# Two block products of the up projection taken from their own pairs and placed earlier, in a fused two-layer encoder kernel

## The chip, the cores and the metric

One core of a Trainium2 chip runs the whole program in one launch. The metric is the time on the device in microseconds (us); the median of several runs counts. TensorE (PE) does the matrix products and its weight loads (PEld); VectorE (DVE), ScalarE (ACT) and GpSimd (POOL) work element by element; SyncE (SP) and POOL issue the transfers (DMA).

## The reference, cut to what matters

Two layers, each with a mixing part (gated linear attention and softmax attention side by side), an output projection, and a gated feed-forward part with a causal convolution of width 3. The change touches the up projection of the feed-forward part:

```python
D_MODEL = 1024; SEQ = 1024; DEPTH = 2; N_META = 16; CONV_W = 3
D_FF = 128 * (-(-8 * D_MODEL // (3 * 128)))        # 2816

def conv_ffn(x, w_up, conv_w, conv_b, w_down):
    h = x @ w_up                                    # (1040, 1024) @ (1024, 2 * 2816)
    L = h.shape[1]
    hp = jnp.pad(h, ((0, 0), (CONV_W - 1, 0), (0, 0)))
    hc = conv_b
    for j in range(CONV_W):
        hc = hc + hp[:, j:j + L] * conv_w[j]
    u, g = jnp.split(hc, 2, axis=-1)
    return (jax.nn.silu(g) * u) @ w_down

def reference(...):
    ...
    for i in range(DEPTH):
        ...
        h = h + jnp.concatenate([o_gla, o_fox], axis=-1) @ w_out[i]
        h = h + conv_ffn(rms_norm(h, ffn_norm[i]), w_up[i], conv_w[i], conv_b[i], w_down[i])
    return rms_norm(h, final_norm)[:, N_META:]
```

## The kernel before, in words

Activations lie with the features on the partitions: eight tiles of 128 features by 1040 positions. Float32 products are made from three matmuls on split operands (mm3, L222 to L224): high weights by high activations, low weights by high activations, high weights by low activations. A split is a cast on ACT (the high half) and a subtraction on DVE (the low half).

The up projection has 22 pairs of column tiles, u and g of 128 columns each. A pair j is a 2 by 2 block product (two halves of the features, two halves of the 1040 positions), done with seven half-size products p = 1 to 7 in place of eight, with sums and differences of blocks as operands. (j, p) below is product p of pair j, both as in the code: pairs count from 0, so the fourth and fifth pair are 3 and 4. One product is 4 feature blocks by 2 pieces of 260 positions by 3 matmuls.

Three things feed a product.

- Its activation operand X[p], shared by all pairs: 4 blocks, each split by put (ACT at L1096, DVE at L1097). X[1] and X[2] are made while the output projection still runs (first_operand, L1140). The others are made inside the up projection by make_t2 (X[6]), make_t3 (X[7]), make_n4 (X[4], L1225), make_t1 (X[5], L1232 and L1233) and make_b22 (X[3]); the table named before says ahead of which index of the sequence each is written out.
- Its weight operand: up_operand and block_operand load the four weight blocks of a pair (SP, L1045), for pairs below 5 also a sum S1 of two blocks, by a load (L1048) and an accumulating transfer of POOL (L1049); other combinations are made on DVE (L1055). up_split makes the high and low half (ACT L1072, DVE L1073). Products 1 and 2 of pair 2 have a load of their own (L1033), as they come before the rest of their pair. ensure(i) writes out the operands up to four products ahead. Even and odd products take their halves from separate pools of three buffers.
- A PSUM place. There are four, of two banks each. place(j, p) says which one a product that begins an accumulation takes; products 6, 7 and 4 accumulate on that of product 1, product 3 on that of product 5.

evacuate takes the results out: of products 1 and 2, the first to come is copied by ACT into a new tile hu (L1262), and the second is added by DVE (L1261); products 6, 7, 4 are copied by ACT; products 5 and 7, then 3, are added by DVE into hg and hu. After product 3 the pair's convolution follows (ACT L1250, four DVE instructions at L1254, a product at L1285), and a transfer of the result by POOL. hu and the other large tiles come from one list of slots; the slot freed longest ago is lent first.

The order of the products is written out in seq, and PE keeps it; the other engines' instructions are put in order by a scheduler when the program is built, and each engine then works through its list in order. The order starts with products 2 and 1 of pairs 0 to 2, then takes pairs 0 and 1 side by side through 6, 7, 4, 5, 3, then the rest of pair 2, and from pair 3 on

```python
        for j in range(3, NFF - 1):
            seq += [(j, 2), (j, 6), (j, 5), (j, 7), (j + 1, 1), (j, 4), (j, 3)]
```

Of the kernel before, what the change touches and what calls it, by code (L numbers as in the profile page):

```python
# [39 lines left out]
M_GK, M_GQ, M_GV, M_GR, M_REM, M_FQ, M_FK, M_FV, M_WO, M_UP = 0, 2, 4, 8, 12, 13, 17, 21, 25, 33  # L40
# [95 lines left out]
class Kern:  # L136
# [891 lines left out]


    def up_operand(self, lyr, j, p, fw, raws, odd):  # L1030
        if j == 2 and p in (1, 2):
            src = fw.tile([128, 4, 128], F32, tag="raw2", name="raw2")
            self.nc.sync.dma_start(src[:], self.wm[lyr, M_UP + 4][:, 4 * p - 4:4 * p, :])  # L1033
            return self.up_split(src, fw, odd)
        return self.block_operand(self.wm[lyr, M_UP + 2 * j], self.wm[lyr, M_UP + 2 * j + 1], 4, j, p, fw, raws, odd, j < N_DMA_SUM)

# [39 lines left out]
    def ffn_up(self, lyr, mix, hT, pp, fw, halves, o0, during_last):  # L1076
# [22 lines left out]


        seq = [(j, p) for j in range(3) for p in (2, 1)] + [(j, p) for p in (6, 7, 4, 5, 3) for j in range(2)]
        seq += [(2, 6), (2, 5), (2, 7), (3, 1), (2, 4), (2, 3)]
        for j in range(3, NFF - 1):
            seq += [(j, 2), (j, 6), (j, 5), (j, 7), (j + 1, 1), (j, 4), (j, 3)]
        seq += [(NFF - 1, p) for p in (6, 5, 7, 2, 4, 3)]

        def place(j, p):
            if p == 1:
                return 3 if j == 2 else j % 2
            if p == 2:  # L1110
                return 2 if j < 3 else 3
            return 0 if j == 1 else 2
        raws, ops = {}, []

# [122 lines left out]
        def make_b22():  # L1237
# [1 line left out]
            for k in range(4):  # L1239
                put(3, k, highk[k][:, t1])  # L1240
            s.put(*highk)
        before = {1: second_half, 2: make_t2, 7: make_t3, 8: make_n4, 10: make_t1, 12: make_b22}


        st = {}
# [47 lines left out]
        for i, (j, p) in enumerate(seq):  # L1293
            ensure(i)
            if i in before:
                before[i]()
            q = st.setdefault(j, {})
            bank, first = {2: "y", 5: "x", 3: "x"}.get(p, "a"), p in (1, 2, 5)
            if first:
                q[bank] = bank2("up", place(j, p))  # L1300
            ps, w = q[bank], ops[i]
            ops[i] = None
            for k in range(4):
                hi_, lo_ = (X[p][e][k // 2].t[:, k % 2, :] for e in range(2))
                for c in range(2):
                    self.mm3(ps[:, c, :n], w[k], (hi_, lo_), c * n, n, first and k == 0, k == 3, not first)
            evacuate(j, p)
            if j == NFF - 1:
                for x in X.pop(p):
                    s.put(*x)  # L1310
                during_last(p)
# [446 lines left out]
```

## Time and profile before

| | |
|---|---|
| median of 3 runs | 2525.41 us (2525.14 to 2525.87) |
| profiled execution, its own time | 2530.31 us |
| its span, first to last instruction | 2528.4 us |
| PE busy in the span | 2483.1 us (98%) |
| DVE busy | 1771.4 us (70%) |
| ACT busy | 1274.4 us (50%) |
| mean granted TensorE clock | 0.996 of full speed |

Times inside the profile count from the first instruction. In a line of a timeline come start, duration, engine, line of the code, operation, tiles written and read, and in brackets the idle time before it with what ended that. In a line of waits come who waited for whom, the sum in us, how often, and the longest. Matmuls overlap in the pipeline, so the distance from one start to the next, not the duration, is the time that a matmul takes. The up projection of layer 0 starts at 568.65 us, that of layer 1 at 1820.19 us.

### The profile page before, as it was taken

The numbers are of one execution on the slowest core, as the hardware profiler recorded it, in microseconds if no ns is written. First come the engines' busy times: TensorE is split into PE (matmuls) and PEld (weight loads), VectorE is DVE, ScalarE is ACT, GpSimd is POOL, SyncE is SP. The second block draws the span as 40 slices with busy tenths as digits, with TensorE's granted clock in tenths as the row PEclk, the third lists the DMA queues.
The fourth block names the chain that finished last, engine by engine and source line by source line (L and its number), as shares of the span: only waits on it lengthen the run. The fifth ranks groups of instructions, "written<-read, shape, count | busy, mean of one in ns | idle before, by whom it ended". The sixth has DMA issues, their size and how long they took to land.

```text
span 2528.4 us, 47014 instructions
## 1 busy us (share of the span) xinstructions
PE 2483.1 (98%) x18442; PEld 2385.4 (94%) x18442; DVE 1771.4 (70%) x3523; ACT 1274.4 (50%) x2733; POOL 385.0 (15%) x567
## 2 busy tenths in 40 slices
PE   9999999999999999999999999999999999999998
PEld 8999999999999999999999899999999999997786
DVE  7656777769877777853666666777797777777545
ACT  7346666645544445641343566665464444455412
POOL 2023433110000000100211334331100000001002
PEclk9999999999999999999999999999999999999999
DMA  3232124342322224763312222143432222257622
GB/s 132 68 87 74 49 88 132 116 140 77 116 81 80 79 76 137 197 168 110 105 58 69 74 80 78 58 152 107 143 92 93 79 85 76 80 159 187 184 74 72
DMA packets 117965, 259.88 MB, mean 103 GB/s; under 512 B 14816, under 2 KB 32480, under 8 KB 117744
## 3 DMA queue, kind: packets, MB, share of 16 engines
q1 hardware_dynamic: 93408, 181.74, 23.1%
q0 software_dynamic: 22464, 72.84, 10.5%
q8 instruction: 144, 2.36, 0.4%
q10 hardware_dynamic: 1872, 2.31, 0.3%
q14 instruction: 77, 0.63, 0.1%
HBM read 176.24 MB, written 67.81 MB: 97 GB/s over the span
## 4 chain that ended last, share of the span: by engine, by line
PE 78%; DVE 14%; ACT 5%; issue 2%; DMA 1%; SPq 0%; DVEq 0%; ACTq 0%
PE up L224 10%; PE up L222 10%; PE up L223 10%; PE mm L222 7%; PE mm L223 7%; PE mm L224 7%; PE down L222 5%; PE down L223 5%; PE down L224 5%; PE av L720 3%; PE tr L694 2%; DVE S L661 2%; DVE x L1097 1%; ACT P L673 1%; PE S L658 1%
## 5 line engine op out<-in xcount | busy, mean ns | idle before, releaser
L222 PE MATMUL up<-x,hi 128*128 128x260 f32 (+1 forms) x2464 | 699.0, 284 | 3.0 <-ACT x L1096 2.4
L224 PE MATMUL up<-x,hi 128*128 128x260 f32 (+1 forms) x2464 | 698.5, 283 | 3.4 <-DVE x L1097 3.4
L223 PE MATMUL up<-x,lo 128*128 128x260 f32 (+1 forms) x2464 | 697.5, 283 | 0.0
L224 PEld LDWEIGHTS up<-x,hi 128*128 128x128 f32 x2464 | 467.3, 190 | 5.2 <-DVE x L1097 5.2
L222 PEld LDWEIGHTS up<-x,hi 128*128 128x128 f32 x2464 | 466.2, 189 | 4.4 <-ACT x L1096 3.2
L223 PEld LDWEIGHTS up<-x,lo 128*128 128x128 f32 x2464 | 466.4, 189 | 0.1
L1073 DVE TENSOR_TENSOR lo<-raw,hi 128x512 fp32r<-128x512 f32 x364 | 247.8, 686 | 170.3 <-ACT hi L1072 170.3
L222 PE MATMUL mm<-xh,hi 128*128 128x348 f32 (+4 forms) x1056 | 363.2, 344 | 0.0
L224 PE MATMUL mm<-xl,hi 128*128 128x348 f32 (+4 forms) x1056 | 339.9, 322 | 0.0
L223 PE MATMUL mm<-xh,lo 128*128 128x348 f32 (+4 forms) x1056 | 339.5, 321 | 0.0
L1072 ACT CAST hi<-raw 128x512 fp32r<-128x512 f32 x364 | 224.7, 620 | 143.7 <-PE up L224 93.3
L222 PEld LDWEIGHTS mm<-xh,hi 128*128 128x128 f32 x1056 | 199.7, 189 | 5.2 <-issue 4.6
L223 PEld LDWEIGHTS mm<-xh,lo 128*128 128x128 f32 x1056 | 199.7, 189 | 0.7 <-issue 0.7
L224 PEld LDWEIGHTS mm<-xl,hi 128*128 128x128 f32 x1056 | 198.6, 188 | 0.4 <-issue 0.3
L189 ACT CAST hi<-raw 128x512 fp32r<-128x512 f32 (+2 forms) x168 | 97.4, 581 | 183.1 <-PE down L224 108.7
L223 PE MATMUL down<-ah,lo 128*128 128x260 f32 (+1 forms) x528 | 169.2, 320 | 0.9 <-DVE lo L191 0.9
L222 PE MATMUL down<-ah,hi 128*128 128x260 f32 (+1 forms) x528 | 168.7, 319 | 0.0
L224 PE MATMUL down<-al,hi 128*128 128x260 f32 (+1 forms) x528 | 168.5, 319 | 0.0
L673 ACT ACTIVATE P<-S,m 116x460 f32<-116x460 f32 (+2 forms) x224 | 124.8, 561 | 71.1 <-DVE m L661 67.4
L337 DVE TENSOR_TENSOR PT<-tr,PT 116x464 fp32r<-116x464 f32 (+3 forms) x240 | 122.9, 515 | 47.2 <-ACT PT L336 45.6
L1055 DVE TENSOR_TENSOR raw<-raw,raw 128x512 f32<-128x512 f32 x198 | 129.5, 685 | 17.4 <-DMA raw<-in_wd_dram 14.9
L1286 POOL DMA_DIRECT2D actd<-cv x44 | 23.6, 535 | 765.1 <-DVE cv L1285 744.2
(289 smaller groups left out, 5621.6 us busy)
## 6 DMA issues: line engine op xcount, KB each, us to landing
raw<-in_wm_dram SPq DMA_DIRECT2D x326, 256.0 KB, 2.7
raw<-in_wd_dram SPq DMA_DIRECT2D x64, 256.0 KB, 3.9
actd<-cv POOLq DMA_DIRECT2D x22, 520.0 KB, 3.0
actd<-cv POOLq DMA_DIRECT2D x22, 512.0 KB, 2.9
cb<-cd SPq DMA_DIRECT2D x16, 520.0 KB, 4.1
st<-actd SPq DMA_DIRECT2D x14, 520.0 KB, 5.1
st<-actd SPq DMA_DIRECT2D x14, 512.0 KB, 5.5
kA<-kA SPq DMA_DIRECT2D x24, 260.0 KB, 4.1
```

Source lines behind the costliest of these rows:

```text
L189: nc.scalar.copy(hi[:, :n, :], raw[:, :n, :])
L222: nc.tensor.matmul(ps, wh, xh[:, c0:c0 + n], start=first, stop=False, skip_group_check=more)
L223: nc.tensor.matmul(ps, wl, xh[:, c0:c0 + n], start=False, stop=False, skip_group_check=more)
L224: nc.tensor.matmul(ps, wh, xl[:, c0:c0 + n], start=False, stop=last, skip_group_check=more)
L337: nc.vector.tensor_tensor(out=lo, in0=src, in1=hi.bitcast(F32), op=ALU.subtract)
L661: nc.vector.tensor_tensor_reduce(out=S[:rows, :n], in0=S[:rows, :n], in1=cb[:rows, c0:k1], scale=1.0, scalar=(BIG if ci == 0 else m[:rows, ...
L673: nc.scalar.activation(P[:rows, :n], S[:rows, :n], AF.Exp, scale=-1.0, bias=m[:rows, nch - 1:nch], accum_out=(den if nch == 1 else d3[:row ...
L694: nc.tensor.transpose(tr[:w, 3 - j, :rows], P[:rows, o:o + w], id_)
L720: nc.tensor.matmul(av[:, a:b], w.rearrange("p a b -> p (a b)"), x, start=(t == ts[0] and part == 0 and i == 0), stop=(t == last and i == 1))
L1055: nc.vector.tensor_tensor(out=q[out][:, :nk, :], in0=q[a][:, :nk, :], in1=q[b][:, :nk, :], op=op)
L1072: nc.scalar.copy(hi[:, :nk, :], src[:, :nk, :])
L1073: nc.vector.tensor_tensor(out=lo[:, :nk, :], in0=src[:, :nk, :], in1=hi[:, :nk, :].bitcast(F32), op=ALU.subtract)
```

## The change

Product 2 of pairs 3 and 4 is taken out of its place in those pairs and put between products of pairs 0 and 1: (3, 2) ahead of (1, 7), and (4, 2) ahead of (1, 4). From (1, 6) on the order is then (1,6), (0,7), (3,2), (1,7), (0,4), (4,2), (1,4), (0,5), (1,5), (0,3), (1,3), and pairs 3 and 4 go straight from product 3 of the pair before to their product 6. The two products get a weight load of their own (so the same block is loaded again with the pair's other blocks), their accumulation takes place 2, and the table before is moved by one or two indices, so that the operands are written out ahead of the same products as before. For these pairs product 2 is now the one that is copied, and product 1 the one that is added.

```diff
     def up_operand(self, lyr, j, p, fw, raws, odd):
-        if j == 2 and p in (1, 2):
+        if (j, p) in ((2, 1), (2, 2), (3, 2), (4, 2)):
             src = fw.tile([128, 4, 128], F32, tag="raw2", name="raw2")
-            self.nc.sync.dma_start(src[:], self.wm[lyr, M_UP + 4][:, 4 * p - 4:4 * p, :])
+            self.nc.sync.dma_start(src[:], self.wm[lyr, M_UP + 2 * j][:, 4 * p - 4:4 * p, :])
             return self.up_split(src, fw, odd)
...
         seq = [(j, p) for j in range(3) for p in (2, 1)] + [(j, p) for p in (6, 7, 4, 5, 3) for j in range(2)]
+        seq.insert(9, (3, 2))
+        seq.insert(12, (4, 2))
         seq += [(2, 6), (2, 5), (2, 7), (3, 1), (2, 4), (2, 3)]
         for j in range(3, NFF - 1):
-            seq += [(j, 2), (j, 6), (j, 5), (j, 7), (j + 1, 1), (j, 4), (j, 3)]
+            seq += ([(j, 2)] if j > 4 else []) + [(j, 6), (j, 5), (j, 7), (j + 1, 1), (j, 4), (j, 3)]
...
             if p == 2:
-                return 2 if j < 3 else 3
+                return 2 if j < 5 else 3
...
-        before = {1: second_half, 2: make_t2, 7: make_t3, 8: make_n4, 10: make_t1, 12: make_b22}
+        before = {1: second_half, 2: make_t2, 7: make_t3, 8: make_n4, 11: make_t1, 14: make_b22}
```

## The prediction

> **What bounds the kernel now.** I read the page first, then the stretches of the two places that the change touches, then the waits and the instruction timeline inside them.
>
> ```profile
> span 2528.4 us, 47014 instructions
> PE 2483.1 (98%) x18442; PEld 2385.4 (94%) x18442; DVE 1771.4 (70%) x3523; ACT 1274.4 (50%) x2733; POOL 385.0 (15%) x567
> PE 78%; DVE 14%; ACT 5%; issue 2%; DMA 1%; SPq 0%; DVEq 0%; ACTq 0%
> ```
>
> TensorE is the bound of the whole: 98% of the span. So a reordering pays only where PE stands still or runs slowly. The chain that ended last nevertheless has 14% of DVE in it, so somewhere PE waits for DVE. The stretches (their length, then busy time and instruction count of PE, PEld, DVE, ACT, POOL, then granted clock, DMA share, GB/s) say where:
>
> ```profile
> 600.15:620.21 20.06, 17.34 (x123) 16.11 (x121) 18.64 (x30) 11.26 (x19) 0.88 (x1) 0.91 0.32 85
> 1852.61:1872.66 20.05, 17.48 (x122) 16.27 (x121) 18.48 (x30) 11.14 (x19) 0.87 (x1) 0.91 0.31 82
> 640.00:680.00 40.00, 40.00 (x337) 40.00 (x336) 31.92 (x42) 20.03 (x29) 1.96 (x3) 1.00 0.39 124
> ```
>
> The third row is steady state: 40.00 us for some 335 matmuls (the edges count two), 0.1195 us each; a block product is 4 blocks x 2 pieces x 3 = 24 matmuls, so 2.87 us. The first two rows (layer 0, layer 1) run from the first matmul of (0,4) to the first of (1,3): five products (0,4), (1,4), (0,5), (1,5), (0,3), 120 matmuls, which at 2.87 would take 14.35 us and take 20.06 and 20.05. **5.7 us are lost in each layer.** What ended the waits there, and what the clock did:
>
> ```profile
> PEld up L224 <- DVE x L1097: 2.3, 4, 0.9
> PE up L224 <- DVE x L1097: 1.5, 3, 0.7
> PE up L222 <- ACT x L1096: 1.2, 2, 0.8
> ```
>
> ```profile
> 612.47 0.59 PE L224 MATMUL up<-x,hi 128*128 128x260 f32 x1 [0.38 <-DVE x L1097]
> 612.86 0.42 PE L222 MATMUL up<-x,hi 128*128 128x260 f32 x1
> 613.50 0.42 PE L222 MATMUL up<-x,hi 128*128 128x260 f32 x1
> 615.46 0.34 PE L222 MATMUL up<-x,hi 128*128 128x260 f32 x1
> 617.33 0.28 PE L222 MATMUL up<-x,hi 128*128 128x260 f32 x1
> ```
>
> PE waits for x, the high and low halves of the operands that make_n4 and make_t1 build on ACT (L1096) and DVE (L1097). (0,5) ends only at 613.50, and from 612.86 to 615.46 twelve matmuls start 0.217 us apart, at half clock. The row at 617.33 starts (0,3). DVE is the cause; it has no pause until its second hg add:
>
> ```profile
> 590.81 1.28 DVE L1073 TENSOR_TENSOR lo<-raw,hi 128x512 fp32r<-128x512 f32 x2
> 592.02 0.68 DVE L1261 TENSOR_TENSOR hu<-up,hu 128x520 f32<-128x520 f32 x1
> 596.87 1.91 DVE L1225 TENSOR_TENSOR h<-h,h 128x520 f32<-128x520 f32 x3
> 602.97 1.42 DVE L1232 SCALAR_TENSOR_TENSOR h<-h,vec,r 128x520 f32<-128x520 f32 x2
> 615.39 0.68 DVE L1261 TENSOR_TENSOR hg<-up,hg 128x520 f32<-128x520 f32 x1
> 617.53 0.70 DVE L1261 TENSOR_TENSOR hg<-up,hg 128x520 f32<-128x520 f32 x1 [0.86 <-PE up L224]
> ```
>
> In a full queue one TENSOR_TENSOR follows the other every 0.61 us (1.28 - 0.68 = 0.60; 1.91 for three), one of L1232 every 0.67 to 0.74.
>
> **The change part by part.** *Matmuls.* Their number is unchanged. Per layer (3,2) and (4,2), 48 matmuls on x2, which has long been complete, move ahead of (1,7) and (1,4): 2 x 2.87 = 5.74 us of work that needs nothing from the late operands. (0,4) then starts 2.87 and (0,5) 5.74 us later than the data forced before. The hole is 5.7. So PE's gain is 5.74 minus the delay of (0,3), and that is set by DVE.
>
> *DVE.* By the built program's order, 26 instructions at 0.61 and four L1232 at 0.67 stand between the first L1225 and the first hg add: 18.5 us, as the rows give (615.39 - 596.87). After the change 28 and four stand there, since low halves of later products now come earlier: 19.7 us. The start moves as well. The two new low halves wait for weights that are now loaded on their own (L1033), into buffers that come free when the low halves of (0,7) and (1,7) are done:
>
> ```profile
> 591.55 0.33 SPq L1045 DMA_DIRECT2D raw<-in_wm_dram  x1
> 593.33 0.33 SPq L1048 DMA_DIRECT2D raw<-in_wm_dram  x1
> raw<-in_wm_dram SPq DMA_DIRECT2D x4, 256.0 KB, 3.0
> 592.22 0.62 ACT L1072 CAST hi<-raw 128x512 fp32r<-128x512 f32 x1
> 594.61 0.59 ACT L1262 COPY hu<-up 128x520 f32<-128x520 f32 x1 [1.77 <-PE up L224]
> ```
>
> The first load takes the place of the one at 591.55 and lands 3.0 us later, at 594.6; cast to 595.2, low half to 595.9; (3,2) starts at 597.3. Covered. The second follows the low half of (1,7), which ends at 592.7 (it trades places with the hu add at 592.02), and lands at 595.8. On ACT stand two casts and the hu copy before and with it, so its cast ends at 596.8 and its low half at 597.5. DVE has four low halves of x7 and two of weights to do until 596.4, then idles some 0.4: the first L1225 starts at 597.4 instead of 596.87. Bounds: 596.4 if the load is early, and later one for one if it is late. Then the hg add starts at 597.4 + 19.7 = 617.1 and ends at 617.8; (0,3), which accumulates on that bank, starts at 617.85 instead of 617.33.
>
> (0,5): four products after 600.15 it starts at 611.63 and needs its last low half with its 21st matmul, at 614.0. On DVE 21 x 0.61 + 4 x 0.67 = 15.5 stand before that: start 612.9, end 613.5. No wait, by 0.5 us. So both kinds of loss in the hole go, the half clock too, as PE no longer pauses: 5.74 - 0.52 = **5.2 us per layer**; 5.7 if the load is early. The second layer's hole has the same length and the same counts.
>
> [...]
>
> *ACT.* Two hu copies of 0.59 come earlier; for these two pairs the copy now follows product 2 and the DVE add product 1, one of each as before. The copy of (4,2) stands ahead of the cast of the last block of x5. It waits for (4,2), done at 608.9, and for its slot, that of acc, read last by the fourth L1232, done at 609.9. It ends at 610.5, while that cast's input comes only at 611.6. (0,5) reuses the same bank, at 611.63. Nothing, with 1.1 us of cover.
>
> *SP and POOL.* Four loads of 256 KB more in all; DMA share is 0.32 there. They stand ahead of the third pair's loads. Its S1 load (593.33) goes behind the low half of (4,2), to 597.5:
>
> ```profile
> 596.95 0.87 POOL L1049 DMA_DIRECT2D raw<-in_wm_dram  x1 [24.86 <-DMA raw<-in_wm_dram]
> raw<-in_wm_dram POOLq DMA_DIRECT2D x1, 256.0 KB, 4.2
> 611.13 0.68 DVE L1055 TENSOR_TENSOR raw<-raw,raw 128x512 f32<-128x512 f32 x1
> ```
>
> so POOL's accumulation starts near 601 and has landed at 606; DVE takes it at about 612. Nothing, with 6 us of cover.
>
> *What comes after.* Pairs 3 and 4 run without their product 2 between (j,3) and (j,6), so three turnarounds get shorter by 2.87: the hu add before (3,6), and bank 2 from (2,3) to (3,5) and from (3,3) to (4,5). DVE must keep up:
>
> ```profile
> 617.00:632.00 15.00, 15.00 (x127) 15.00 (x127) 13.91 (x15) 9.78 (x12) 0.56 (x1) 1.00 0.17 43
> 632.00:650.00 18.00, 18.00 (x153) 18.00 (x152) 18.00 (x24) 10.95 (x16) 1.98 (x3) 1.00 0.46 141
> 650.00:663.30 13.30, 13.30 (x114) 13.30 (x113) 10.39 (x16) 7.05 (x11) 0.00 (x0) 1.00 0.56 180
> 619.39 1.30 DVE L1254 SCALAR_TENSOR_TENSOR cv<-hg,vec,cv 128x1039 f32<-128x1039 f32 x1 [0.56 <-ACT cv L1250]
> 632.65 0.69 DVE L1073 TENSOR_TENSOR lo<-raw,hi 128x512 fp32r<-128x512 f32 x1
> 634.61 0.28 PE L222 MATMUL up<-x,hi 128*128 128x260 f32 x1
> ```
>
> Before, the low half of (2,4) ends at 633.34, 1.3 us ahead of its product. After, (2,4) starts at about 635.0 (617.85 + 6 x 2.87). From the first L1254 at 619.4 on (the two low halves already made are missing, the convolutions of pairs 0 and 1 are the same, 1.21 each) the built order puts that low half at 633.2 in layer 0 and, with both pairs' convolutions ahead of it, at 634.3 in layer 1: 1.8 and 0.7 us to spare. The same sum gives (2,3) 0.9, and the add that frees bank 2 for (3,5) 0.8. All small, none negative, so I take zero; the upper bound is a rival. Behind 650 DVE idles again (10.39 of 13.30).
>
> Sum: 2 x 5.2 = 10.4 us off 2530.3 (the profiled execution's own time; span 2528.4), so 2519.9 there. The median of the runs shown is 2525.41, 4.9 us lower; the hole is work and waits on engines, so I take the same 10.4 off it: **2515.0**. If all 5.7 come back in each layer, 2514.0. A difference of 0.2%, 5 us, is about what a measurement of this kernel can tell from none.
>
> **The rivals.** *DVE gives part of it back later.* PE reaches (4,6), at 663.3 before, 5.2 us sooner in each layer, with the same DVE work; DVE's idle time from 617 to there is 1.09 + 2.91 = 4.0, most of it at the end. Spare 0.7 to 0.9 at three places is within what my sum can miss: 0.1 us at each of the waits for ACT on the way would be over a microsecond. Price 1 to 2.5 us per layer: 2517 to 2520. Against it: DVE reaches 619.4 no later than before. 0.15.
>
> *The half clock stays.* If the pauses did not cause it, twelve matmuls at 0.217 instead of 0.1195 cost 1.2 us per layer wherever they fall: 2517.4. For it: no pause there is above 0.9 us. Against it: the fall follows four pauses in 5 us, and the stretch without pauses shows 1.00. 0.08. [...]
>
> *Slower: ACT and DVE queue up behind the load of (4,2).* The cast for it stands in front of every cast of x4 and x5, its low half in front of all of make_n4 and make_t1, and DVE has no idle time, so each microsecond beyond 595.8 delays the hole's end by one. It decides at 3.0 + 5.2 = 8.2 us to landing; at 11 us it is 2525.4 + 2 x 2.8 = 2531. Against it: 3.0 in this stretch, two loads at a time. 0.04.
>
> *The products fill nothing,* because (0,5) waits for the bank that (4,2) used, or (0,3) for its add, as long as it waited for x: no change, 2525. 0.04.
>
> **How the numbers follow.** The forecast, 0.69, holds 2513.8 to 2516.5. With the first two rivals the range reaches to 2520, which leaves out 0.08 and the edges. Faster by over 0.2%: forecast, half clock and most of the giving back, 0.89; within it 0.06; slower 0.05.
>
> **What would show it.** Right: between (0,4) and (1,3), now six products, PE waits under 0.5 us and the granted clock stays at 1.00; (0,3) starts near 617.9; the first L1225 near 597.4; no PE wait for lo L1073 or hu L1261 up to (4,6). Wrong: waits of PE for DVE adds L1263 (the same lines, moved by two) or lo L1073 between 630 and 660, or a first L1225 after 599.

## The result

The changed kernel takes 2517.62 us (median of 6 executions, 2515.66 to 2519.32), beside 2525.91 us for the kernel before in the same comparison (6 executions, 2525.14 to 2527.37): ratio 0.9966, 95% interval 0.9954 to 0.9979. It is faster by some 8.6 us, within 5.3 to 11.6. The profiled execution of the changed kernel took 2517.71 us, span 2515.8. In its code everything above line 1101 keeps its number; what was L1225, L1232, L1254 and L1261 is now L1227, L1234, L1256 and L1263.

The page after:

```profile
span 2515.8 us, 47034 instructions
PE 2475.8 (98%) x18442; PEld 2380.5 (95%) x18442; DVE 1771.1 (70%) x3523; ACT 1274.3 (51%) x2733; POOL 386.1 (15%) x567
PE 83%; DVE 9%; ACT 5%; issue 1%; DMA 1%; SPq 0%; DVEq 0%; POOL 0%; ACTq 0%; POOLq 0%
```

The counts of PE, DVE and ACT are the same. The share of DVE in the chain that ended last went from 14% to 9%; that is over 100 us, about ten times the gain, so it says that the chain now runs through PE for longer, and not how much time was saved. The stretches from the first matmul of (0,4) to the first of (1,3), layer 0, then layer 1, and a stretch behind them, in the kernel after (length, busy time and count of PE, PEld, DVE, ACT, POOL, granted clock, DMA share, GB/s):

```profile
602.76:620.28 17.52, 17.52 (x147) 17.33 (x145) 17.52 (x29) 11.79 (x20) 0.88 (x1) 1.00 0.49 112
1848.72:1866.03 17.31, 17.31 (x146) 17.31 (x145) 17.31 (x29) 11.90 (x20) 0.87 (x1) 1.00 0.46 114
633.00:663.00 30.00, 30.00 (x253) 30.00 (x253) 29.32 (x40) 17.53 (x25) 1.98 (x3) 1.00 0.49 150
```

Six products now lie there, 6 x 2.87 = 17.22 us of matmuls, so 0.30 and 0.09 us are lost where 5.7 were, and the clock stays at 1.00. The only wait of PE left between 597 and 625 us, and the instructions around it:

```profile
PEld up L222 <- DVE hg L1263: 0.2, 1, 0.2
```

```profile
594.85 2.05 DVE L1073 TENSOR_TENSOR lo<-raw,hi 128x512 fp32r<-128x512 f32 x3
596.81 1.91 DVE L1227 TENSOR_TENSOR h<-h,h 128x520 f32<-128x520 f32 x3
...
616.52 0.70 DVE L1263 TENSOR_TENSOR hg<-up,hg 128x520 f32<-128x520 f32 x1
617.27 0.39 PE L222 MATMUL up<-x,hi 128*128 128x260 f32 x1
```

The last row starts (0,3), straight behind the hg add's end at 617.22. The view shows no idle time of DVE from the first L1227 to that add: 616.52 - 596.81 = 19.71 us, for the 28 and 4 instructions counted at 19.7. Behind it, from 633 to 663 us, DVE is busy 29.32 of 30.00 us and PE all 30.00: nothing is given back.

A longer measure takes the shift of the products out: from the first matmul of the up projection to the first of (5,6), by when both kernels have done the same products. In the profiled execution of before that is 114.72 and 115.91 us (layers 0 and 1), in that of after 109.12 and 110.35: 5.6 less in each layer, 11.2 in all. The two spans differ by 12.6; the other 1.4 us lie outside and are no part of the change, as the further profiles below show.

### The profile page after: what moved, and what is told of

It is laid out like the page before. It is cut to its first block, busy times and chain, and to the rows that moved or that the text cites. A ratio compares the mean times of both kernels' runs of the same rounds, so it can differ in the third digit from the quotient of the medians.

```text
span 2515.8 us, 47034 instructions
## 1 busy us (share of the span) xinstructions
PE 2475.8 (98%) x18442; PEld 2380.5 (95%) x18442; DVE 1771.1 (70%) x3523; ACT 1274.3 (51%) x2733; POOL 386.1 (15%) x567
## 3 DMA queue, kind: packets, MB, share of 16 engines
q0 software_dynamic: 22464, 72.84, 10.4%
## 4 chain that ended last, share of the span: by engine, by line
PE 83%; DVE 9%; ACT 5%; issue 1%; DMA 1%; SPq 0%; DVEq 0%; POOL 0%; ACTq 0%; POOLq 0%
PE up L222 11%; PE up L224 11%; PE up L223 11%; PE mm L222 7%; PE mm L224 7%; PE mm L223 7%; PE down L222 5%; PE down L223 5%; PE down L224 5%; PE av L720 3%; PE tr L694 2%; DVE S L661 1%; PE S L658 1%; PE wo L222 1%; PE wo L224 1%
```

## The experiments

**The two kernels once more.** The changed kernel and the kernel before, without an edit.

> The changed kernel once more, timed against the kernel before on one chip. If the hole between (0,4) and (1,3) is what moved (11.2 us of PE standing still or at half clock, both layers together, in the traces), the ratio comes nearer to 1 - 11/2526 = 0.9956 than the 0.9967 of the first timing. If part of the 12.6 us between the two profiled executions was an odd execution of the kernel before, it stays near 8 us (0.9967).

> The kernel before against itself, with a second profile. Ratio 1.000 within 0.001. The theory of the hole: five products from the first matmul of (0,4) take 20.0 to 20.1 us again in each layer, where 14.35 is the pace. If the hole of the first profile was an odd execution, it is 1 us shorter or more here.

After: 2517.98 us beside 2527.95 (27 executions of before), ratio 0.9961, interval 0.9948 to 0.9973. That lies halfway between the 0.9956 and the 0.9967 of the two cases, and the interval holds both, so the times do not decide between them. Before against itself: 2527.48, ratio 1.0000, interval 0.9992 to 1.0009. The stretches of after look the same again, (0,4) to (1,3) in layers 0 and 1:

```profile
602.75:620.23 17.48, 17.48 (x146) 17.31 (x145) 17.48 (x29) 11.78 (x20) 0.88 (x1) 1.00 0.46 114
1849.32:1866.71 17.39, 17.39 (x146) 17.39 (x145) 17.39 (x29) 11.84 (x20) 0.87 (x1) 1.00 0.47 116
```

Those of before do not. First the two stretches, then the 3.4 us before, in and after the half clock of layer 0:

```profile
599.05:619.20 20.15, 17.45 (x123) 16.23 (x121) 18.61 (x30) 11.22 (x19) 0.88 (x1) 0.92 0.31 84
1851.34:1870.14 18.80, 16.20 (x122) 14.80 (x121) 18.67 (x30) 11.40 (x20) 0.87 (x1) 1.00 0.34 87
608.50:611.90 3.40, 1.81 (x10) 1.39 (x11) 3.40 (x7) 2.52 (x5) 0.00 (x0) 1.00 0.21 72
611.90:615.30 3.40, 3.40 (x18) 3.40 (x17) 3.40 (x7) 0.00 (x0) 0.88 (x1) 0.51 0.24 83
615.40:618.80 3.40, 3.40 (x30) 3.40 (x30) 1.86 (x4) 2.23 (x3) 0.00 (x0) 1.00 0.55 77
```

In layer 1 PE waited as long, but the clock stayed at 1.00, and the stretch took 18.80 us instead of 20.15. So there are two losses: waits for x, 18.80 - 14.35 = 4.45 us, and a half clock that comes on top in some executions, here 1.35 us. The prediction had them as one. In that layer 1 (0,3) starts at 1867.15, 0.05 us behind the end of the first hg add, so DVE's list already set it; in the first profile, with the half clock, it started at 617.33, 1.26 us behind the end of that add at 616.07. How often the second comes was the question of three more single profiles.

> The kernel before, one more profiled execution. Open: of 10.4 us, how much of the gain is waiting for x, which before pays in every execution, and how much is the half clock, seen in three of four such stretches so far and in none of the 16 with a product put in. Theory (the half clock comes in some executions at the same place, near 612 and 1864 us, and costs 1.2 us there): the first matmul of (0,4) to that of (1,3) takes 20.1 us with it and 18.8 without; from the first matmul of the up projection to that of (5,6) 115.0 to 115.9 with, about 114 to 115 without; everything else in the span is 2296 +- 1. Rival (the half clock only delays matmuls that would have waited for DVE anyway, so it costs nothing): 20.1 either way.

> As for the run before it: 20.1 us with half clock, 18.8 without by the theory; 20.1 either way by the rival.

> The changed kernel, one more profiled execution: no half clock between the first matmul of the up projection and that of (5,6) in either layer, (0,4) to (1,3) 17.3 to 17.6 us with six products in it, first matmul to (5,6) 109 to 110.7, and the rest of the span 2296 +- 1, so a span of 2515 to 2517. If the half clock is chance and not tied to the pauses, it shows up here too in one of the stretches, with 1.7 us more.

The kernel before, first of these profiles, then the second:

```profile
598.70:618.55 19.85, 17.41 (x123) 16.07 (x121) 18.65 (x30) 11.25 (x19) 0.88 (x1) 0.91 0.32 85
1849.72:1868.53 18.81, 16.23 (x123) 14.82 (x121) 18.68 (x30) 11.41 (x20) 0.87 (x1) 1.00 0.33 84
```

```profile
598.82:618.92 20.10, 17.38 (x123) 16.15 (x122) 18.64 (x30) 11.25 (x19) 0.88 (x1) 0.92 0.30 82
1850.75:1870.79 20.04, 17.46 (x123) 16.25 (x121) 18.48 (x30) 11.13 (x19) 0.87 (x1) 0.91 0.29 80
```

After:

```profile
601.22:618.78 17.56, 17.53 (x146) 17.32 (x145) 17.56 (x29) 11.79 (x20) 0.88 (x1) 1.00 0.49 116
1847.85:1865.25 17.40, 17.40 (x146) 17.39 (x145) 17.40 (x29) 11.83 (x20) 0.87 (x1) 1.00 0.40 105
```

In four profiles of before, 6 of 8 stretches have the half clock (19.85 to 20.15 us) and 2 have not (18.80, 18.81): the theory's two lengths, and not the rival's one. Up to (5,6) the half clock costs less than in the stretch: in layer 1 it is 115.89 us on average with it and 114.92 without, and layer 0, with it, took 114.51 and 114.76 in these two, somewhat under the 115.0 expected. In the profiles of all kernels that put a product or two in here (after three times, and the six below), 18 stretches, it comes in none. Over the four profiles the stretch of before loses 5.4 us on average, that of after, over three, 0.2. From the first matmul of the up projection to (5,6), before takes 114.75 and 115.40 us on average, after 109.17 and 110.51: **5.6 and 4.9 us, 10.5 in all**, and the mean spans, 2526.35 and 2515.83, differ by 10.5 too. Some 1.5 to 1.8 us of that are the half clock (1.0 to 1.2 us in 3 of 4 stretches, twice; an estimate from these eight), the rest is waiting. The whole gain lies in this part of the two layers: what is left of the spans, expected at 2296 +- 1, was 2294.6 (0.4 under the band) and 2296.7 in the two of before and 2295.6 in after. The last of these, after_3, with a span of 2515.3, has a mean granted clock of 0.997 over the span, with 1.00 in both stretches above: what half clock it has lies outside them.

**One product alone.** Only (3,2) early, and only (4,2) early; the load of its own, the place and the table follow.

```diff
# only32
+        seq.insert(9, (3, 2))
-            seq += [(j, 2), (j, 6), ...
+            seq += ([(j, 2)] if j > 3 else []) + [(j, 6), ...
# only42
+        seq.insert(11, (4, 2))
-            seq += [(j, 2), (j, 6), ...
+            seq += ([(j, 2)] if j != 4 else []) + [(j, 6), ...
```

> Only (3,2) is moved, (4,2) stays in its pair. Theory (PE work fills a wait whose end DVE sets, and without long pauses the clock holds): PE has one product of 2.87 us to fill with; DVE's list up to the first hg add has 27 + 4 instructions (26 + 4 before, 28 + 4 with both), so (0,3) starts 0.5 us earlier than before, at about 616.8, with one more product done: 3.4 us per layer, 6.8 in all, 2519. Rival (the half clock comes whatever the pauses): 1.1 us per layer less, 2521. Rival (the gain is not the hole): nothing near half of the whole change's.

> Only (4,2) is moved, (3,2) stays in its pair. The same sums: it lies behind (0,4), so the 0.6 us that (0,4) loses stay, while (0,5) starts 2.87 us later than before; DVE again 27 + 4. By the theory the end of the hole is DVE's, so it does not matter where in front of (0,5) the filling stands: 3.4 us per layer as with (3,2) alone, 2519. If filling worked only at the place of its own wait, it would be 0.6 us per layer less than (3,2) alone.

(3,2) alone: 2523.04 us, ratio 0.9980 (0.9971 to 0.9989). (4,2) alone: 2523.72, ratio 0.9983 (0.9974 to 0.9992). So 4.9 us (2.7 to 7.4) and 4.2 us (2.1 to 6.5), where 6.8 was expected of each: for (3,2) the interval holds that and the half-clock rival's 4.6 alike, for (4,2) the expected 6.8 lies outside it. Up to (5,6) layers 0 and 1 take 111.36 and 112.17 with (3,2), 6.6 us less than before's average, and 111.69 and 113.02 with (4,2), 5.4 less. The first is what was expected. The second is 1.2 less, and that is the figure of the rival by which filling works only at the place of its own wait (0.6 per layer). The traces show another cause: in both kernels (0,3) starts 0.05 to 0.06 us behind the end of the first hg add, and DVE's list up to that add is equally long (19.0 to 19.1 us from the first L1226), but with (4,2) alone the list starts 0.31 and 0.68 us later after the layer's first matmul. Part of that, in layer 1, is a wait of DVE for the cast of a weight shortly ahead of it:

```profile
1845.11 0.69 DVE L1073 TENSOR_TENSOR lo<-raw,hi 128x512 fp32r<-128x512 f32 x1 [0.26 <-ACT hi L1072]
```

This rests on one profile of each. That of (4,2) was the slowest of its 11 executions, 2527.84 us; its half clocks lie in other stages: the granted clock is 1.00 in both stretches below, and 0.91, 0.84, 0.89 and 0.89 from 450 to 470, 1120 to 1130, 1700 to 1715 and 2370 to 2385 us. (0,4) to (1,3), with (3,2), where five products lie in it, then with (4,2), where there are six:

```profile
601.47:618.17 16.70, 15.41 (x122) 14.58 (x121) 16.62 (x27) 10.71 (x18) 0.88 (x1) 1.00 0.39 100
1849.47:1866.00 16.53, 15.34 (x123) 14.59 (x122) 16.47 (x26) 10.79 (x18) 0.87 (x1) 1.00 0.35 96
```

```profile
599.88:619.46 19.58, 18.12 (x147) 17.46 (x146) 19.58 (x32) 13.20 (x22) 0.88 (x1) 1.00 0.40 95
1849.95:1869.78 19.83, 17.79 (x146) 17.37 (x145) 19.79 (x33) 13.22 (x22) 0.88 (x2) 1.00 0.31 82
```

Some 2.2 to 2.6 us of waiting is left (16.70 - 14.35; 19.58 - 17.22) of the 4.45 without half clock in before: each fills about 2 us, its 2.87 less the 0.6 by which DVE's list grew. With one product put in the granted clock is already 1.00 in all four stretches. So the two gains, 6.6 and 5.4, add up to more than the 10.5 of both: each is credited with the same half clock.

**Products that do nothing.** The order of before, with two products put in whose result is never read. This says whether PE's time is really to be had here.

```diff
         for i, (j, p) in enumerate(seq):
...
+            if i in (9, 11):
+                fill = bank2("fill", 2)
+                for k in range(4):
+                    hi_, lo_ = (X[2][e][k // 2].t[:, k % 2, :] for e in range(2))
+                    for c in range(2):
+                        self.mm3(fill[:, c, :n], ops[i][k], (hi_, lo_), c * n, n, k == 0, k == 3)
```

> The order of before is kept, with product 2 of pairs 3 and 4 in its place; ahead of (1,7) and of (1,4) stand two added products of 24 matmuls whose result is never read, 96 matmuls of additional PE work in the whole kernel (96 x 0.1195 = 11.5 us), no other engine gets anything. Theory (PE waits for x in this place, 4.3 us per layer without the half clock and 5.7 with it): each layer's 5.74 fill that wait, PE comes out 0.2 to 1.4 us later and never at half clock between (0,7) and (1,3): about +1 us without the half clock in before, -1 with it, so 2524.5 to 2527.5 beside a before of 2525.9. Rival (PE is the bound and its time is the number of its matmuls): +11.5 us, 2537. If it is the theory, then what after gained is that these products' time is had for nothing here, and nothing else.

2529.16 us beside 2527.61, ratio 1.0009 (1.0001 to 1.0018): 11.5 us of added matmuls cost 1.6 us by the medians and 2.3 by the ratio (0.3 to 4.5), where up to 1.6 was expected. The rival's +11.5 is out. Up to (5,6) the layers take 114.77 and 116.89 us, beside 114.75 and 115.40 in before: nothing in layer 0, 1.5 in layer 1, where (0,6) ahead of the first added product already waits longer for x6. The stretches:

```profile
602.71:619.92 17.21, 17.21 (x146) 17.21 (x145) 17.21 (x29) 10.85 (x18) 0.88 (x1) 1.00 0.39 108
1855.09:1872.41 17.32, 17.32 (x147) 17.32 (x145) 17.32 (x28) 11.08 (x18) 0.87 (x1) 1.00 0.40 108
```

These are after's figures, with the fourth and fifth pair untouched. So the moved products are done for nothing, and what after gains is their time, 11.5, taken out of steady state, less the little that does not fit.

**What ends the stretch now.** After, with the low half of each block of x5 written twice, 2.4 us more of DVE per layer, in make_t1.

```diff
                 nc.vector.tensor_tensor(out=y, in0=x, in1=y, op=ALU.subtract)
                 put(5, k, y)
+                hi_, lo_ = (X[5][i][k // 2].t[:, k % 2, :W] for i in range(2))
+                nc.vector.tensor_tensor(out=lo_, in0=y, in1=hi_.bitcast(F32), op=ALU.subtract)
```

> After, with the four low halves of X[5] written twice in make_t1: 4 x 0.61 = 2.4 us more on DVE per layer, PE's work unchanged. Theory (after still ends this stretch by DVE's list, whose slack at (0,5) is at most 0.5 us and at the hg add ahead of (0,3) none): (0,5) waits about 1.9 us, (0,3) starts 2.4 later in each layer, +3.8 to +4.9 us in all, 2521.4 to 2522.5. Rival (after is PE-bound here, DVE has spare time): no change, 2517.6, and no PE wait for x.

2522.04 us beside 2527.61, ratio 0.9979 (0.9970 to 0.9988), where after had 0.9961 against the same kernel: about 4.5 us slower than after, as the theory said. Stretches and the waits of PE in the first:

```profile
603.18:623.08 19.90, 17.95 (x147) 17.40 (x145) 19.90 (x33) 12.47 (x20) 0.88 (x1) 1.00 0.41 95
1850.88:1870.71 19.83, 17.93 (x146) 17.46 (x145) 19.83 (x33) 12.48 (x20) 0.88 (x1) 1.00 0.37 92
```

```profile
PEld up L224 <- DVE x L1238: 1.5, 1, 1.5
PEld up L222 <- DVE hg L1265: 0.8, 1, 0.8
```

(0,5) takes 1.7 us longer in both layers, so its slack in after was about 0.7. (0,3) starts 51.29 us after the layer's first matmul instead of 48.84, and 52.33 instead of 49.75: the whole 2.4 to 2.6, so there the slack is nil. The first wait is at L1238, the added instruction. After is still tied to DVE's list at the end of the stretch; the fill is used up exactly.

**The slower rival.** After, with the load of (4,2) sent twice into the same tile.

```diff
-            self.nc.sync.dma_start(src[:], ...)
+            for _ in range(2 if j == 4 else 1):
+                self.nc.sync.dma_start(src[:], ...)
```

> After, with the load of (4,2) issued twice into the same tile, the second behind the first's end, so that it lands about 3.0 us later. Theory of the prediction's slower rival (ACT's and DVE's lists stand behind this load, and DVE waited about 0.4 us for it in after): the first L1227 and (0,3) come 2.6 to 3.0 us later in each layer, +5 to +6 us in all, 2523 to 2524. Rival (the scheduler has put enough ahead of the low half of (4,2), so the load is covered): no change, 2517.6.

2518.54 us, ratio 0.9964 (0.9951 to 0.9978): as after. The theory, +5 to +6, falls; the second load did land 2.8 us later in layer 0 (598.23, in after 595.46). DVE's instructions around the first L1228 (L1227 in after, where all three low halves came ahead of it):

```profile
595.01 1.29 DVE L1074 TENSOR_TENSOR lo<-raw,hi 128x512 fp32r<-128x512 f32 x2
596.21 1.92 DVE L1228 TENSOR_TENSOR h<-h,h 128x520 f32<-128x520 f32 x3
598.04 1.31 DVE L1098 TENSOR_TENSOR x<-h,x 128x520 fp32r<-128x520 f32 x2
599.26 0.69 DVE L1074 TENSOR_TENSOR lo<-raw,hi 128x512 fp32r<-128x512 f32 x1
```

The scheduler, which knew of the second load, put the low half of (4,2) five instructions later, and the first L1228 starts at 596.21, 0.6 earlier than in after; that low half ends at 599.95, and its product starts at 605.84 in this profile: 5.9 us to spare. In layer 1 the load landed at 1845.24, and there DVE did wait for it:

```profile
1845.91 0.69 DVE L1074 TENSOR_TENSOR lo<-raw,hi 128x512 fp32r<-128x512 f32 x1 [0.63 <-ACT hi L1073]
```

(0,3) starts 50.41 us after that layer's first matmul instead of 49.75 to 49.99. So the changed order took up the later load in layer 0 whole and in layer 1 but for about half a microsecond: the slower rival's mechanism is there, at a tenth of its price. A load that is late without the scheduler knowing would meet the order of after; that wasn't tried.

**An earlier place for (3,2).** In after (0,6) still waits for x6. (3,2) is taken ahead of it.

```diff
-        seq.insert(9, (3, 2))
+        seq.insert(6, (3, 2))
-        before = {1: second_half, 2: make_t2, 7: make_t3, 8: make_n4, 11: make_t1, 14: make_b22}
+        before = {1: second_half, 2: make_t2, 8: make_t3, 9: make_n4, 11: make_t1, 14: make_b22}
```

> After, with (3,2) ahead of (0,6) in place of (1,7), its operand written out ahead of make_t3, so make_t3 comes later in DVE's list by one low half. In after (0,6) waits 0.1 to 0.3 us for x6 in layer 0 and 0.9 to 1.1 in layer 1; the product covers that wait. Theory (DVE's list sets the end of the whole stretch; PE's own waiting ahead of it is repaid there): (0,6) starts without a wait, but (0,3) comes no earlier than in after by more than 0.4 us per layer, so 2517 to 2518, no difference that can be told. Rival (waits of PE add up one by one): 0.1 + 1.0 = 1.1 us faster, 2516.5. A loss, if its load, now first of the two, lands late: (0,6) would wait for x6 or (3,2) for its low half.

2518.30 us, ratio 0.9964 (0.9951 to 0.9976): no difference from after that can be told. The interval holds the rival's 1.1 us as well; the traces decide. Layer 1's wait of PE ahead of (0,4), in after, and then its wait at the end of the stretch, in this kernel:

```profile
PEld up L224 <- DVE x L1097: 0.8, 1, 0.8
```

```profile
PEld up L222 <- DVE hg L1263: 0.8, 1, 0.8
```

The wait is gone at (0,6) and has come back in front of (0,3), which starts 49.06 and 49.84 us after the layer's first matmul, in after 48.84 and 49.75. That is the theory, by one profile: DVE's list sets the end of the stretch, and what PE saves ahead of it is repaid there.

## Why the prediction was right

The change is faster, by the mechanism forecast: two products on x2 do their 5.74 us in each layer where PE waited for x. **The size** was 10.4 us of 2525.41, a ratio of 0.9959; the two comparisons gave 0.9966 and 0.9961, with 0.9959 inside both intervals, and the profiles 10.5. The 2517.6 us measured lie above the 2513.8 to 2516.5 of the forecast itself, inside the range to 2520 that the first two rivals had added; by the time alone the rival of the half clock, 2517.4, was the nearer one, and only the traces tell them apart. Of the 2.6 us above 2515.0, 0.5 are the base, 2525.91 in the same comparison in place of 2525.41. The gain there was 8.3 us by the medians, and 10.0 in the second comparison (2527.95 and 2517.98). What is left of the ratio, 0.2 to 0.7 thousandths, the measurement can't tell from nothing.

**Two terms were off and offset each other.** The half clock was counted in every stretch; it was there in 6 of 8, which takes 0.25 x 1.2 = 0.3 us off the gain per layer (the six average 20.04 us, the two others 18.81). The delay left at (0,3) was put at 0.52 us; the stretches of after lose 0.2. It was 0.52 only because the half clock had already pushed (0,3) back to 617.33; in layer 1 without the half clock (0,3) starts 1.4 us later in after than in before (49.86 us after the first matmul on average, 48.48 before), by DVE's list. The forecast of 5.2 per layer stands beside 5.6 and 4.9; that it is so near is luck.

**DVE's list.** The first L1225 was forecast at 597.4, after an idle 0.4 for the load of (4,2); it came at 596.81 (layer 0 began 0.22 us earlier too), with some 0.1 of waiting: the load landed at 595.46 instead of 595.8, its cast ended at 596.17 instead of 596.8, and the row of three low halves, the last of them that of (4,2), lasts 2.05 us where three in a full queue last 1.91. The length of the list, 19.7, was right to 0.01 us, so the hg add came at 616.52 instead of 617.1, and (0,3) at 617.27 instead of 617.85. (0,5), without a wait, had 0.7 us of slack instead of 0.5. The mis-sized step is the wait for the load and its cast.

**Half clock.** That it goes with the pauses is borne out: 6 of 8 stretches with all of them, none of 18 with a part or the whole filled. The longest pause does not tell the two apart: 0.80 us in layer 0 of before, with it, 0.79 in layer 1 of before_again, without it. Why the one has it and the other not was not shown; the last section has the figures.

**The rivals.** DVE gave nothing back: no wait of PE for DVE or ACT from 620 to 680 us, though DVE was full, 29.32 of 30.00 us; the 0.7 to 0.9 of slack, taken as zero cost, held. The half clock did not stay: the granted clock is 1.00 in both stretches of all three profiles of after. The load of (4,2) was just in time, and when it was made later by the plan, the order gave way for the most part; I had treated the order as fixed. The products filled what they were to fill.

## What to carry to other kernels

Where one engine bounds the kernel and still stands still in one place, look for its own work that needs nothing from the late engine, and put it there; a product whose result is never read tells in one run how much room there is. Then count the late engine's list once more: the fill is worth its length only up to the point at which that list ends, and any more of it is repaid there. A loss seen in one profile should be looked for in a second before it is counted in every execution.

## What the hardware showed beside this

In the profiled execution of before the half clock comes four times inside the kernel, from 38.71, 458.55, 612.15 and 1864.84 us on, each time for 3.41 us. The two in the up projection, each behind the 3.41 us ahead of it:

```profile
608.74:612.15 3.41, 1.76 (x8) 1.13 (x8) 3.41 (x7) 3.05 (x7) 0.00 (x0) 1.00 0.00 0
612.15:615.56 3.41, 3.09 (x14) 3.09 (x15) 3.41 (x7) 0.31 (x1) 0.38 (x1) 0.50 0.45 154
1861.43:1864.84 3.41, 1.53 (x9) 0.90 (x8) 3.41 (x7) 3.04 (x6) 0.00 (x0) 1.00 0.09 16
1864.84:1868.25 3.41, 3.41 (x16) 3.41 (x17) 3.41 (x6) 0.00 (x0) 0.25 (x1) 0.50 0.46 143
```

PE was busy for 1.76 and 1.53 us of the 3.41 ahead of them. In before_again the pauses of PE for x in layer 1, without the half clock (granted clock 1.00 from 1851.34 to 1870.14 us), are the same as those of the profiled execution of before in layer 0, which has it from 612.2:

```profile
1859.87 0.39 PE L222 MATMUL up<-x,hi 128*128 128x258 f32 x1 [0.41 <-ACT x L1096]
1861.10 0.39 PE L224 MATMUL up<-x,hi 128*128 128x258 f32 x1 [0.72 <-DVE x L1097]
1862.62 0.39 PE L222 MATMUL up<-x,hi 128*128 128x258 f32 x1 [0.79 <-ACT x L1096]
```

```profile
608.81 0.39 PE L222 MATMUL up<-x,hi 128*128 128x260 f32 x1 [0.42 <-ACT x L1096]
610.04 0.39 PE L224 MATMUL up<-x,hi 128*128 128x260 f32 x1 [0.72 <-DVE x L1097]
611.58 0.39 PE L222 MATMUL up<-x,hi 128*128 128x260 f32 x1 [0.80 <-ACT x L1096]
```

So the same pauses, the longest 0.80 and 0.79 us, come with it or without, and what decides between the two no run here shows. In the stretches of dve4, with single waits of 1.5 and 0.8 us, the granted clock stayed at 1.00.
